# Two gate projections as seven half-size products each, with weight factors made in the first scan and the first gate as a pass of its own

## The chip, the core and the metric

The kernel runs on one core of a Trainium2 chip. The metric is the device time of one execution in microseconds (us). Engines are named as the profile does: PE is TensorE, PEld its weight loads, DVE is VectorE, ACT is ScalarE, POOL is GpSimd, SP the engine from whose queue all DMAs of this kernel are issued.

## What is computed

One layer of a mixer with two parallel recurrent branches over 16 meta tokens and 2048 tokens of width 1024, in float32. Cut to what matters here:

```python
h = concat([meta_tokens, x])                  # 2064 x 1024
xn = rmsnorm(h, norm_w)
proj = xn @ w_in                              # 1024 x 6152
a_q, a_k, a_v, a_beta, a_alpha, a_z, b_q, b_f, b_i, b_g, gate_a, gate_b = split(proj)
y_a = gated_delta_net(conv(a_q, a_k, a_v), a_beta, a_alpha) * silu(a_z)   # 4 heads of 128, chunked scan
y_b = hgrn2(b_q, b_f, b_i) * silu(b_g)                                    # 4 heads of 128, chunked scan
mixed = sigmoid(gate_a) * (y_a @ w_branch_a) + sigmoid(gate_b) * (y_b @ w_branch_b)
out = rmsnorm(h + mixed @ w_out, final_norm_w)[16:]
```

`gate_a` and `gate_b` are two projections of 1024 columns each from the same normalised tokens.

## The kernel before

Tokens are worked on in 17 chunks of 128; chunk 0 holds the meta tokens, the 16 others go in 8 pairs. Each float32 operand of a projection is kept as two float16 tiles, a high and a low part, and a product is three matmuls per block of 128 rows: high by high, high by low, low by high (`SPLITS`, L251). A projection of 512 columns for one chunk is then 8 x 3 = 24 matmuls into one PSUM bank (`tok_major`, L253).

The work runs in three stages.

- **First scan** (L708 to L749): normalise and transpose the tokens of a pair (`xprep`) and store them in device memory (`xs_d`, L712); run the second branch's recurrence (`levels`, `scan1`) with its four projections. In it the generator `bg` prepares the weights for the second scan, two steps per chunk (L744), placed behind marks of the scan's own instructions by `issue_after`.
- **Second scan** (L1056 to L1102): convolution and recurrence of the first branch, one `stage` and one `scan2` per chunk, both with raised priority (`AHEAD`).
- **Merges** (L1183): per chunk two branch products (`branch`, L797), the scaled sum, a split into float16 parts, transposes, the output product (L1172) and the last norm.

Weights are prepared by `prepare` (L221): load 2 MB, take a scale from the largest squares (`stats_steps`, L185), then in 8 steps (`split_steps`, L204) scale on VectorE, copy the high part on ScalarE (L216) and subtract it on VectorE or GpSimd (L217). They lie in a ring of six buffers, tag `w`, which also holds the two pair tiles of the second scan.

The gates are made in the third place, for every chunk by itself: `gate` (L353) takes two projections of 512 columns per gate, and ScalarE applies tanh as it takes the bank (L360). Their four weights are begun in the last pairs of the second scan (L1072, L1077, L1085). The gates of chunks 1 to 3 are made at the end of that scan (in pieces of 256 columns), and their first branch right after it (L1103); the merge loop makes the gates of a chunk three chunks ahead (L1186). The weights of the branches and of the output product are prepared around the end of the second scan (L1102, L1124 to L1127).

Instructions are written in program order with priorities. A scheduler orders each engine's queue by a simulated timeline; on the chip each queue then runs in that order, and an instruction that waits holds up those behind it. PSUM tags of the second and third stage: `d`, `e`, `s`, `o` with two banks each (`BANKS`, L32); gate products use `d`, branches `e`, transposes and output products `s`.

## Time and profile before

| | |
|---|---|
| runs | 1903.33, 1904.47 and 3626.0 us, median 1904.47 |
| profiled execution | 1903.0 us, span of its instructions 1901.2 us |
| TensorE busy | 1774.5 us, 93%, 17247 matmuls |
| VectorE busy | 1202.5 us, 63% |
| ScalarE busy | 881.9 us, 46% |
| GpSimd busy | 311.6 us, 16% |
| mean granted clock of TensorE | 0.973 |
| DMA | 105 MB, 55 GB/s in the mean |

The page gives the busy share of each engine and of 40 equal slices of the span (digits are tenths). Groups of instructions are named by line, engine, operation and tiles, with count, total and mean duration. The chain is followed back from the last instruction to what released each step. Windows give the busy time of each engine in a stretch, with the clock that TensorE was granted as a share of 2.4 GHz. TensorE's matmuls overlap, so the distance between starts says more of their cost than their duration.

### The profile page before, as it was taken

The page shows a single profiled execution, that of the slowest core. Times are in us where ns is not written, and L with a number is a line of the kernel's source. Part 1 is how long each engine was busy: PE and PEld are TensorE (multiplying, and loading weights), DVE is VectorE, ACT ScalarE, POOL GpSimd, SP SyncE. Part 2 cuts the span into 40 slices and gives each one's busy share as a digit, 9 for nine tenths or more (in the row PEclk, how much of TensorE's full clock was granted, in tenths as well). Part 3 has the DMA queues.
Part 4 walks back from the last instruction along what each step waited for, and adds up shares of the span by engine and source line. Part 5 has one row for each costly group of instructions (what it writes and reads, how often), then busy time and mean ns, then how long its engine had stood idle before and what let it go on. Part 6 is the DMA issues. An engine that isn't in the chain of part 4 may idle for free.

```text
span 1901.2 us, 43142 instructions
## 1 busy us (share of the span) xinstructions
PE 1774.5 (93%) x17247; PEld 1215.1 (64%) x17247; DVE 1202.5 (63%) x5070; ACT 881.9 (46%) x2208; POOL 311.6 (16%) x441
## 2 busy tenths in 40 slices
PE   4599999999986899999999998888999999999998
PEld 3476767777665788788888876764444444444444
DVE  7954765667579788988988989758222333242344
ACT  7654665566576445655556686753111111111111
POOL 3300111112115212212212145322000000000000
PEclk9699999999988899999999998999999999999999
DMA  9111111010300001000000132240111111211011
GB/s 334 41 50 41 57 52 52 13 46 35 118 30 12 29 24 35 24 29 30 13 29 11 56 115 93 76 153 25 67 56 34 61 50 39 72 45 34 33 51 45
DMA packets 38733, 105.05 MB, mean 55 GB/s; under 512 B 4156, under 2 KB 4340, under 8 KB 35460
## 3 DMA queue, kind: packets, MB, share of 16 engines
q1 hardware_dynamic: 38532, 102.29, 15.4%
q8 instruction: 135, 2.21, 0.5%
q14 instruction: 66, 0.54, 0.1%
HBM read 77.12 MB, written 25.17 MB: 54 GB/s over the span
## 4 chain that ended last, share of the span: by engine, by line
PE 70%; DVE 17%; ACT 7%; issue 3%; DMA 1%; POOL 1%; SPq 0%; ACTq 0%; POOLq 0%; DVEq 0%
PE pgate L259 16%; PE pc L267 10%; PE pout L1172 9%; PE pbr L806 7%; PE pq L267 5%; PE pzg L259 4%; PE pi L259 3%; PE pg L259 3%; DVE wsc L213 3%; DVE pair L318 2%; PE pkq L869 1%; PE pl L576 1%; DVE Y L901 1%; DVE R L899 1%; POOL yp L639 1%
## 5 line engine op out<-in xcount | busy, mean ns | idle before, releaser
L259 PEld LDWEIGHTS <-x 128*128 128x128 f16 x3192 | 311.4, 99 | 256.3 <-issue 8.4
L259 PE MATMUL pgate<-w_ga,x 128*128 128x512 f16 (+1 forms) x912 | 179.3, 352 | 6.6 <-POOL w_ga L217 2.8
L259 PE MATMUL pgate<-w_gb,x 128*128 128x512 f16 (+1 forms) x912 | 170.2, 345 | 0.0
L1172 PE MATMUL pout<-w_o,mt 128*128 128x512 f16 (+1 forms) x792 | 169.3, 373 | 0.2 <-ACT mt L1160 0.2
L318 DVE SCALAR_TENSOR_TENSOR pair<-raw,cw,pair 128x256 f32<-128x256 f32 (+1 forms) x297 | 140.5, 500 | 3.0 <-ACT pair L312 2.2
L806 PEld LDWEIGHTS <-y 128*128 128x128 f16 x768 | 75.5, 99 | 93.9 <-issue 8.3
L1172 PEld LDWEIGHTS <-mt 128*128 128x128 f16 x792 | 77.3, 98 | 88.6 <-DVE mt L1162 0.5
L1174 DVE SCALAR_TENSOR_TENSOR hres<-pout,mm,hres 128x512 f32<-128x512 f32 (+1 forms) x33 | 24.2, 734 | 165.3 <-PE pout L1172 165.3
L806 PE MATMUL pbr<-w_bra,y 128*128 128x512 f16 x384 | 89.7, 384 | 4.4 <-DVE mix L808 2.0
L259 PE MATMUL pi<-w_bi,x 128*128 128x512 f16 x408 | 92.5, 379 | 0.0
L267 PE MATMUL pq<-x,w_bq 128*128 128x256 f16 x768 | 89.2, 276 | 0.0
L267 PEld LDWEIGHTS <-w_aq 128*128 128x128 f16 x864 | 77.0, 100 | 16.8 <-POOL w_aq L217 4.5
L259 PE MATMUL pg<-w_bg,x 128*128 128x512 f16 x384 | 87.7, 379 | 0.0
L806 PE MATMUL pbr<-w_brb,y 128*128 128x512 f16 x384 | 87.4, 382 | 0.0
L267 PEld LDWEIGHTS <-w_ak 128*128 128x128 f16 x864 | 76.6, 98 | 13.7 <-issue 2.8
L553 DVE TENSOR_TENSOR QK<-QK,Tb 128x1024 f32<-128x1024 f32 x48 | 61.0, 1270 | 36.9 <-PE pl L581 36.9
L267 PEld LDWEIGHTS <-w_av 128*128 128x128 f16 x864 | 76.6, 99 | 12.0 <-issue 1.7
L901 DVE TENSOR_TENSOR Y<-Y,R 128x2 f32<-128x2 f32 (+14 forms) x510 | 83.9, 197 | 0.0
L267 PEld LDWEIGHTS <-w_bq 128*128 128x128 f16 x768 | 76.1, 99 | 9.4
L899 DVE TENSOR_TENSOR R<-R,U 128x2 f32<-128x2 f32 (+14 forms) x510 | 81.5, 193 | 0.3
L267 PE MATMUL pq<-x,w_bf 128*128 128x256 f16 x672 | 79.9, 273 | 0.0
L1175 ACT ACTIVATE mix<-hres 128x512 f32<-128x512 f32 x22 | 13.8, 629 | 129.2 <-DVE hres L1174 82.3
(470 smaller groups left out, 3672.7 us busy)
## 6 DMA issues: line engine op xcount, KB each, us to landing
x<-xs_d SPq DMA_DIRECT2D x14, 1024.0 KB, 4.7
hx<-in_x_dram SPq DMA_DIRECT2D x16, 512.0 KB, 3.4
xs_d<-x SPq DMA_DIRECT2D x8, 1024.0 KB, 3.9
hres<-in_x_dram SPq DMA_DIRECT2D x16, 512.0 KB, 3.5
out_dram<-hres SPq DMA_DIRECT2D x16, 512.0 KB, 2.6
yb_d<-yt SPq DMA_DIRECT2D x16, 256.0 KB, 2.0
ya_d<-yt SPq DMA_DIRECT2D x16, 256.0 KB, 2.0
y<-ya_d SPq DMA_DIRECT2D x16, 256.0 KB, 2.6
```

The lines of the kernel that those rows point to most:

```text
L213: E.tensor_scalar(t, raw[:, k, :], rows[:, k:k + 1], sc[:, 0:1], ALU.mult, ALU.mult)
L259: T.matmul(po[:, j:j + cols], xt[:, k, xa, c0:c0 + P], wt[:, k, wa, j:j + cols], start=(n == 0), stop=(n == 23))
L267: T.matmul(po, wt[:, k, wa, h * P:(h + 1) * P], xt[:, k, xa, c0:c0 + ncol], start=(n == 0), stop=(n == 23))
L318: V.scalar_tensor_tensor(av, rows(h, j), wv(j), av, ALU.mult, ALU.add)
L553: V.tensor_tensor(qk, qk, dv, ALU.mult)
L576: T.matmul(pd[a:a + 32, 2 * h + i], K[:, a:a + 32], Q[:, a:a + 32].rearrange("p (m z t) -> p m z t", z=2, t=s)[:, :, 1], start=True, stop= ...
L639: G.tensor_tensor(yp[:, 1], y, yp[:, 0], ALU.subtract)
L806: T.matmul(pb, y[:, h, xa, :], w[0][:, 4 * i + h, wa, :], start=(n == 0), stop=(n == 11))
L899: V.tensor_tensor(R[:, e, c:], R[:, e, c:], U[:, e, c:c + 1].broadcast_to([P, n // 2, 16 - c]), ALU.mult)
L901: V.tensor_tensor(Y[:, e, c:], Y[:, e, c:], R[:, e, c:], ALU.add)
L1172: T.matmul(po, mt[:, xa, k, :], wo[i][0][:, k, wa, js], start=(n == 0), stop=(n == 23))
L1174: V.scalar_tensor_tensor(h[:, i, js], po, mm[:, 2 + i:3 + i], h[:, i, js], ALU.mult, ALU.add)
```

## The change

Each gate of a pair of chunks (256 tokens by 1024 by 1024) is cut in two along all three sizes, and the four blocks of the result are put together from seven products of 128 tokens by 512 by 512 (Strassen's scheme in Winograd's form) instead of eight. Each product is 4 x 3 = 12 matmuls into one bank.

- `gate_steps` makes seven weight factors per gate from the four blocks of its weight and stores them in device memory (`wg_d`). Its steps run in the first scan, three per chunk from the second pair on, beside the two of `bg`. The raw weight is loaded twice (once for the scale), into one buffer of 1 MB.
- `left` makes the four sums of the token blocks for a pair, stores them (`ss_d`) in the first gate's pass and loads them in the second gate's.
- `gate_pair` runs seven products; ScalarE takes the first bank, VectorE adds the others into four float32 blocks, and ScalarE applies tanh in place.
- `first_gate` runs for the first gate: pairs 0 and 1 in the last two chunks of the second scan, pairs 2 to 7 after it, with nine steps of the four last weights behind each. The results go to device memory (`ga_d`). The merges load them again.
- `second_gate` runs in the merge loop, one pair ahead. The early gates and the early branches of chunks 1 to 3 fall away.

```diff
-    def gate(c, xt, which, t, parts=(0, 1)):
-        c0 = ((c - 1) % 2) * P
-        for i in parts:
...
-            tok_major(pg, xt, c0, wsl[n][0], 256 if c < 4 else 512)
-            A.activation(t[:, i, :], pg, AF.Tanh, scale=hu[:, j:j + 1])
+    def gate_steps(i, off, pool):
+        src = w_in[0][:, off:off + D].rearrange("(a k p) (b n) -> p k a b n", a=2, p=P, b=2)
...
+        def load(k):
+            t = gx.tile([P, 2, 2, 512], F32, tag="t8", name="graw")
+            for a in range(2):
+                SY.dma_start(t[:, a], src[:, k, a])
+            return t
+        for k in range(4):
+            t = load(k)
...
+            if k % 2:
+                V.tensor_reduce(st, t.rearrange("p a b n -> p (a b) n"), AX.X, ALU.max, apply_absolute_value=True)
...
+            else:
+                for j in range(4):
...
+                    A.activation(junk, t[:, j // 2, j % 2], AF.Square, scale=rows[:, j // 2, k:k + 1],
+                                 accum_out=st[:, j:j + 1])
+            yield
...
+        for k in range(4):
+            t = load(k)
+            for a in range(2):
+                A.activation(t[:, a], t[:, a], AF.Copy, scale=fac[:, a, k:k + 1])
+            def put(n, b, f):
+                o = pool.tile([P, 2, 512], F16, tag="go", name="go", bufs=3)
+                A.activation(o[:, 0], b, AF.Copy, scale=f)
+                if f == 1.0:
+                    V.tensor_tensor(o[:, 1], b, o[:, 0], ALU.subtract)
+                else:
+                    V.scalar_tensor_tensor(o[:, 1], b, f, o[:, 0], ALU.mult, ALU.subtract)
+                SY.dma_start(wg_d[i][:, ORDER.index(n), k], o)
...
+            put("P1", b11, 1.0)
+            put("P2", b21, 1.0)
+            put("P3", b22, 2.0)
+            yield
+            V.tensor_tensor(b11, b12, b11, ALU.subtract)
+            put("P5", b11, 2.0)
+            V.tensor_tensor(b12, b22, b12, ALU.subtract)
+            put("P7", b12, 2.0)
+            yield
+            V.tensor_tensor(b22, b22, b11, ALU.subtract)
+            put("P6", b22, 2.0)
+            V.tensor_tensor(b21, b21, b22, ALU.subtract)
+            put("P4", b21, 1.0)
+            yield
+    def left(q, first):
+        x = xpair(q)
+        S = mp.tile([P, 4, 4, 2, P], F16, tag="xm", name="xs", bufs=2)
+        if not first:
+            SY.dma_start(S, ss_d[q])
+            return x, S
...
+        def put(n, s):
+            A.activation(S[:, n, :, 0], s, AF.Copy, scale=0.5)
+            V.scalar_tensor_tensor(S[:, n, :, 1], s, 0.5, S[:, n, :, 0], ALU.mult, ALU.subtract)
...
+        V.tensor_tensor(s, a(1, 0, 0), a(1, 1, 0), ALU.add)
+        V.tensor_tensor(t, a(1, 0, 1), a(1, 1, 1), ALU.add)
+        V.tensor_tensor(s, s, t, ALU.add)
+        put(0, s)
+        for h in range(2):
+            V.tensor_tensor(s, s, a(0, 0, h), ALU.subtract)
+        put(1, s)
+        for h in range(2):
+            V.tensor_tensor(s, a(0, 1, h), s, ALU.subtract) if h == 0 else V.tensor_tensor(s, s, a(0, 1, h), ALU.add)
+        put(3, s)
+        u, t = tmp("s3"), tmp("s3l")
+        G.tensor_tensor(u, a(0, 0, 0), a(1, 0, 0), ALU.subtract)
+        G.tensor_tensor(t, a(0, 0, 1), a(1, 0, 1), ALU.subtract)
+        G.tensor_tensor(u, u, t, ALU.add)
+        put(2, u)
+        SY.dma_start(ss_d[q], S)
+        return x, S
+    def gate_pair(i, xS, w, t):
...
+        def prod(n):
+            po = psd("pgate")
+            m = 0
+            for k in range(4):
+                for (xa, wa) in SPLITS:
+                    T.matmul(po, L[n](k, xa), w[ORDER.index(n)][:, k, wa], start=m == 0, stop=m == 11)
+                    m += 1
+            return po
+        def add(po, *ds):
+            with tc.high_priority(offset=OFS):
+                for d, s in ds:
+                    V.tensor_tensor(d, s, po, ALU.add)
+        def end(d):
+            A.activation(d, d, AF.Tanh, scale=hu[:, i:i + 1])
+        po = prod("P1")
+        with tc.high_priority(offset=OFS):
+            A.activation(c21, po, AF.Copy)
+        add(prod("P2"), (c11, c21))
+        end(c11)
+        add(prod("P6"), (c12, c21))
+        add(prod("P7"), (c21, c12))
+        add(prod("P5"), (c12, c12), (c22, c21))
+        end(c22)
+        add(prod("P3"), (c12, c12))
+        end(c12)
+        add(prod("P4"), (c21, c21))
+        end(c21)
+    def first_gate(q):
...
+        gate_pair(0, left(q, True), wga, t)
+        for j in range(2):
+            SY.dma_start(ga_d[2 * q + 1 + j], t[j])
...
                         run_steps(bg, LAST[i] if last else 2)
+                        if not last:
+                            run_steps(gsteps, 3)
             if p == 0:
+                gsteps = chain(gate_steps(0, OFF_GA, p1), gate_steps(1, OFF_GB, p1))
...
                         if p == NP_ - 2:
-                            run_steps(bg, 13)
-                            bg2 = gate_begin("gb0")
+                            wga = [f for j in range(4) for f in gate_part(0, j, wp if j < 3 else gx)]
                 else:
-                    bg3 = gate_begin("gb1")
-                    run_steps(bg2)
...
+                    first_gate(i)
...
+        wgb = gate_part(1, 0, wp)
+        bg = chain(prepare(beg["bra"], "bra", ((), EVEN)), prepare(beg["brb"], "brb", ((), EVEN)),
+                   prepare(beg["o0"], "o0", (HALF, EVEN)), prepare(beg["o1"], "o1", (HALF, EVEN)))
+        for q in range(2, NP_):
+            first_gate(q)
+            run_steps(bg, 9)
+        run_steps(bg)
+        wgb += [f for j in (1, 2, 3) for f in gate_part(1, j, wp if j < 3 else gx)]
...
+        def second_gate(q):
+            gate_pair(1, left(q, False), wgb, [tbs[:, (2 * q + j) % 4] for j in range(2)])
+        def merge(c, tb):
+            mix = raw_t("mix").rearrange("p h i -> p (h i)")[:, :D].rearrange("p (a n) -> p a n", a=2)
+            SY.dma_start(mix, ga_d[c])
+            branch(c, ya_d, wba, mix)
...
-        for c in range(1, NCH):
-            merge(*ready.pop(0))
-            if c + 3 < NCH:
-                ready.append(gates(c + 3))
+        second_gate(0)
+        for q in range(NP_):
+            if q + 1 < NP_:
+                second_gate(q + 1)
+            for j in range(2):
+                merge(2 * q + 1 + j, tbs[:, (2 * q + j) % 4])
```

`gate_part(i, j, pool)` loads two of the stored factors (one for the last j) into a buffer of the ring `w`, or into the buffer of `gate_steps` for the last. The factors lie in the order P1, P2, P6, P7, P5, P3, P4. The branch inputs `y` have two buffers instead of three.

## Rows read from the trace of the kernel before

**Rows 1.** The page's part 1, TensorE; part 2, TensorE in 40 slices.
```profile
PE 1774.5 (93%) x17247; PEld 1215.1 (64%) x17247; DVE 1202.5 (63%) x5070; ACT 881.9 (46%) x2208; POOL 311.6 (16%) x441
...
PE   4599999999986899999999998888999999999998
```
**Rows 2.** The page's part 4, the chain that ended last, by line.
```profile
PE pgate L259 16%; PE pc L267 10%; PE pout L1172 9%; PE pbr L806 7%; PE pq L267 5%; PE pzg L259 4%; PE pi L259 3%; PE pg L259 3%; DVE wsc L213 3%; DVE pair L318 2%; PE pkq L869 1%; PE pl L576 1%; DVE Y L901 1%; DVE R L899 1%; POOL yp L639 1%
```
**Rows 3.** Pieces of that chain, 1440 to 1485 us: start, us, what.
```profile
1445.91 10.36 PE pgate L259 x48
1456.27 0.89 PE mT L1158 x16
```
**Rows 4.** Windows: stretch, length, busy us (count) of the engines, clock, DMA.
```profile
1120.00:1320.00 200.00, 174.59 (x1490) 127.73 (x1489) 162.67 (x681) 120.90 (x310) 77.43 (x87) 0.93 0.26 92
...
1335.00:1850.00 515.00, 515.00 (x2530) 239.37 (x2529) 152.78 (x320) 75.83 (x122) 0.00 (x0) 1.00 0.15 50
1850.00:1901.20 51.20, 42.31 (x242) 22.03 (x239) 25.81 (x64) 8.45 (x16) 0.00 (x0) 0.97 0.11 42
```
**Rows 5.** Windows of 60 us in the first scan, one pair each.
```profile
130.00:190.00 60.00, 60.00 (x871) 43.60 (x870) 29.03 (x78) 30.79 (x59) 4.30 (x3) 1.00 0.12 42
...
370.00:430.00 60.00, 59.25 (x849) 43.59 (x842) 38.21 (x116) 37.45 (x77) 8.91 (x7) 1.00 0.10 37
430.00:490.00 60.00, 56.80 (x842) 41.78 (x840) 40.34 (x112) 35.69 (x71) 13.26 (x9) 1.00 0.17 63
```
**Rows 6.** Groups by line with shapes apart, ScalarE; then line 200's instructions.
```profile
L406 ACT ACTIVATE x<-hx,rx 128x1024 f16<-128x1024 f32 x17 | 19.6, 1164 | 5.1 <-DVE rx L403 5.1
...
L200 ACT ACTIVATE junk<-w_gb,nw 128x512 f16<-128x512 f32 x16 | 11.6, 722 | 1.4 <-DMA w_gb<-in_w_in_dram 1.4
...
L216 ACT ACTIVATE w_gb<-wsc 128x512 f16<-128x512 f32 x16 | 9.8, 624 | 3.9 <-DVE wsc L213 3.8
...
L200 ACT ACTIVATION_READ_ACCUMULATOR junk<-w_ga,nw x16: 185/188/213, 1084.3 to 1106.6; 128x1 f32 x16
```
**Rows 7.** Timeline of VectorE at 1273 us: start, us, instruction.
```profile
1273.25 0.68 DVE L217 TENSOR_TENSOR w_bra<-wsc,w_bra 128x512 f16<-128x512 f32 x1
1273.85 0.15 DVE L195 TENSOR_TENSOR stats<-stats 128x2 f32<-128x2 f32 x1
```
**Rows 8.** Waits of TensorE, 190 to 490 us: total, times, longest.
```profile
PE yT L643 <- ACT yp L638: 3.3, 2, 1.7
PE pl L581 <- DVE QK L553: 3.2, 4, 1.0
```
**Rows 9.** DMA issues: size and median us to landing.
```profile
w_ga<-in_w_in_dram SPq DMA_DIRECT2D x4, 1024.0 KB, 7.3
```
**Rows 10.** Windows of w_ga's, then w_gb's instructions: PE, DVE, ACT, POOL.
```profile
1085.00:1260.00 175.00, 40.52 (x288) 6.48 (x8) 22.19 (x46) 22.79 (x24) 0.94 0.25 90
...
1085.00:1260.00 175.00, 31.69 (x274) 9.62 (x16) 22.33 (x48) 18.65 (x16) 0.94 0.25 90
```
**Rows 11.** Windows of pgate's (PE, ACT), then pbr's (PE, DVE) instructions.
```profile
1120.00:1320.00 200.00, 84.31 (x624) 8.19 (x12) 0.93 0.26 92
...
1120.00:1320.00 200.00, 35.50 (x144) 7.61 (x12) 0.93 0.26 92
```
**Rows 12.** Line 217, two of its groups: ns min/median/max, first to last start.
```profile
L217 POOL TENSOR_TENSOR w_o<-wsc,w_o x8: 1155/1246/1467, 1289.0 to 1310.0; 128x512 f16<-128x512 f32 x8
L217 DVE TENSOR_TENSOR w_o<-wsc,w_o x8: 671/681/1653, 1289.2 to 1309.3; 128x512 f16<-128x512 f32 x8
```
**Rows 13.** Timeline of VectorE in one merge.
```profile
1414.69 1.29 DVE L1143 SCALAR_TENSOR_TENSOR mix<-tb,us,mix 128x1024 f32<-128x1024 f32 x1
...
1424.36 0.69 DVE L1162 COPY mt<-mT 128x1024 f16<-128x1024 f16 x1 [4.06 <-PE mT L1158]
```
**Rows 14.** Windows of 50 and of 10 us, for the clock.
```profile
450.00:500.00 50.00, 47.21 (x733) 32.38 (x732) 29.64 (x56) 23.16 (x50) 11.31 (x7) 1.00 0.26 97
...
1130.00:1140.00 10.00, 6.36 (x25) 5.04 (x24) 9.61 (x53) 6.36 (x19) 6.17 (x7) 0.66 0.00 0
```

More of the change, by code (lines that the diff above doesn't have):

```diff
@@ L30 @@
 AHEAD = 1500
-EARLY = 3
 BANKS = (dict(d=3, e=2, s=2, o=1), dict(d=2, e=2, s=2, o=2))
@@ L160, in load_small, with scale_of @@
         return cw, gna, gnb, hb
-    def scale_of(stats, nt, tag):
+    def scale_of(stats, nt, tag, exp=WS_EXP):
         sc = cp.tile([P, 2], F32, name=f"sc_{tag}")
@@ L247, in hybrid_kernel @@
     yb_d = [dp.tile([P, H, 2, P], F16, name=f"yb_d{c}") for c in range(NCH)]
+    wg_d = [dp.tile([P, 7, 4, 2, 512], F16, name=f"wg_d{i}") for i in range(2)]
+    ss_d = [dp.tile([P, 4, 4, 2, P], F16, name=f"ss_d{q}") for q in range(NP_)]
+    ga_d = [dp.tile([P, 2, 512], F32, name=f"ga_d{c}") for c in range(NCH)]
     uy = cp.tile([P, 2], F32, name="uy")
@@ L278, in hybrid_kernel @@
     G.memset(hist, 0.0)
-    hu = cp.tile([P, 4], F32, name="hu")
+    hu = cp.tile([P, 2], F32, name="hu")
     def conv(n, xt, pidx, dst, later=False, tag=None):
@@ new lines, in gate_part, with a, tmp @@
+    def gate_part(i, j, pool):
+        n = 2 if j < 3 else 1
+        t = pool.tile([P, 2 * 4, 2, 512] if n == 2 else [P, 4, 2, 512], F16, tag="w" if n == 2 else "t8", name=f"wg{i}{j}")
+        SY.dma_start(t.rearrange("p (f k) a n -> p f k a n", k=4), wg_d[i][:, 2 * j:2 * j + n])
+        return [t[:, 4 * f:4 * f + 4] for f in range(n)]
+    def left(q, first):
[4 more added lines that the diff above has]
+            return x, S
+        def a(i, j, h):
+            return x[:, 4 * j:4 * j + 4, h, P * i:P * i + P]
+        def put(n, s):
+            A.activation(S[:, n, :, 0], s, AF.Copy, scale=0.5)
+            V.scalar_tensor_tensor(S[:, n, :, 1], s, 0.5, S[:, n, :, 0], ALU.mult, ALU.subtract)
+        def tmp(n):
+            return sp.tile([P, 512], F32, tag="st", name=n).rearrange("p (k i) -> p k i", k=4)
+        s, t = tmp("s1"), tmp("s1l")
+        V.tensor_tensor(s, a(1, 0, 0), a(1, 1, 0), ALU.add)
[15 more added lines that the diff above has]
+        return x, S
@@ L364, in hybrid_kernel @@
+    def first_gate(q):
+        t = [raw_t("gt0").rearrange("p h i -> p (h i)")[:, :D], acc_t("gt1")]
+        t = [x.rearrange("p (a n) -> p a n", a=2) for x in t]
+        gate_pair(0, left(q, True), wga, t)
+        for j in range(2):
+            SY.dma_start(ga_d[2 * q + 1 + j], t[j])
     bw = gp.tile([P, KT, 2, 2 * H], F16, name="bw")
@@ L1051, in xpair_mid @@
                 return xpair(p)
-            t = mp.tile([P, KT, 2, 2 * P], F16, tag="xm", name="xm")
+            t = mp.tile([P, KT, 2, 2 * P], F16, tag="xm", name="xm", bufs=2)
             SY.dma_start(t, xs_d[p])
@@ L1070, in hybrid_kernel @@
                         conv("q", xn, p + 2, pn["q"])
-                        if p == NP_ - 2:
-                            bg = chain(gate_begin("ga0"), gate_begin("ga1"))
                     else:
@@ L1112, in hybrid_kernel @@
         SY.dma_start(fnw, final_norm_w.rearrange("(o d) -> o d", o=1).broadcast_to([P, D]))
-        def gates(c):
-            if c % 2 == 1:
-                xg[c] = xg[c + 1] = xpair((c - 1) // 2)
-            t = gate_tiles(c)
-            for w in range(2):
-                gate(c, xg[c], "ab"[w], t[w])
-            return c, *t
-        beg["o0"], beg["o1"] = out_begin(0, wx), out_begin(1, wx)
-        run_steps(prepare(beg["brb"], "brb", ((), EVEN)))
-        wba, wbb = wsl["bra"], wsl["brb"]
-        run_steps(prepare(beg["o0"], "o0", (HALF, EVEN)))
-        run_steps(prepare(beg["o1"], "o1", (HALF, EVEN)))
-        wo = [wsl["o0"], wsl["o1"]]
+        beg["bra"] = br_begin(w_branch_a, gna, "bra")
+        beg["brb"] = br_begin(w_branch_b, gnb, "brb")
+        beg["o0"], beg["o1"] = out_begin(0, wx), out_begin(1, wx)
+        wgb = gate_part(1, 0, wp)
[6 more added lines that the diff above has]
+        wgb += [f for j in (1, 2, 3) for f in gate_part(1, j, wp if j < 3 else gx)]
+        tbs = wp.tile([P, KT, 2, 512], F16, tag="w", name="tbs")
+        tbs = tbs.rearrange("p k a n -> p (k a n)").bitcast(F32).rearrange("p (c a n) -> p c a n", c=4, a=2)
+        wba, wbb, wo = wsl["bra"], wsl["brb"], [wsl["o0"], wsl["o1"]]
         us = p1.tile([P, 4], F32, name="us")
@@ L1134, in hybrid_kernel @@
             V.tensor_scalar(uo[:, i:i + 1], wo[i][1], XS / MS, None, ALU.mult)
-        def merge(c, mix, tb):
-            if c > EARLY:
-                branch(c, ya_d, wba, mix)
+        def second_gate(q):
[4 more added lines that the diff above has]
+            branch(c, ya_d, wba, mix)
             h = acc_t("hres").rearrange("p (a n) -> p a n", a=2)
```

69 lines of the change are left out of this document (25 added, 44 removed).

## The prediction

> **What bounds the kernel now.** I read the page's engine shares first: TensorE is busy 93% of the span, VectorE 63%, and the slices show TensorE at 9 nearly everywhere except at the start, around 600 us and around 1150 to 1320 us [rows 1]. In the chain that ended last the lines with the largest shares are all TensorE's, the gate product (L259) first [rows 2]. Busy TensorE is not TensorE at its peak, so next come the pieces of that chain in the last third: 48 matmuls of 512 columns take 10.36 us, 215.8 ns each, and they follow one another without a gap [rows 3]. From 1335 to 1850 us TensorE is busy 515.00 of 515 us at clock 1.00 [rows 4]: here each matmul left out is worth its 215.8 ns.
>
> Between 1120 and 1320 us it is otherwise: TensorE is idle for 25.4 us of 200 and granted 0.93 of its clock, which costs some 14 us more, while VectorE works 162.7 us of it [rows 4]. I call these 39 us the lost time of the seam between second scan and merges. In the first scan a pair of chunks takes 60 us; the pair without weight preparation beside it leaves TensorE no idle time, the five after it 1.9 us each on average (0.75 in the best of the five, 3.2 in the last), with VectorE busy near 39 us and ScalarE near 36 [rows 5].
>
> **The change part by part.** *Matmuls removed.* Each gate of a pair of chunks was 2 chunks x 2 halves x 24 = 96 matmuls of 512 columns; seven half-size products of 12 make 84. Over 8 pairs and 2 gates that is 1536 against 1344, and 192 x 0.2158 = 41.4 us go. (The first three chunks ran as 256 columns, twice as many; I count them as the same columns.) The gates take 331.5 us of TensorE now and 290.1 after, 18.13 us per gate and pair.
>
> *Weight factors in the first scan.* Per gate: 8 loads of 1 MB (each part twice, as two DMAs), then per part 2 scalings of 1024 elements on ScalarE, 7 copies there, and 11 VectorE operations of 512 (4 differences, 7 second halves). ScalarE: 8 squares of 0.72 + 0.19, 4 x (2 x 1.16 + 7 x 0.63) [rows 6], together 34 us. VectorE: 44 x 0.60 (start to start in a run without gaps [rows 7]; an operation alone is shown at 0.68; no sum of two f16 tiles into f32 is in the trace, I take the f32 ones') + 2 reductions of 2048 elements at 4 x 0.60 each + small ones, some 33 us. Both gates: ScalarE +68, VectorE +66. The 32 steps are issued three per chunk from the second pair on, so spread over 5.5 pairs: per 60 us VectorE goes from 39 to 51, ScalarE from 36 to 48. Neither is full, so no throughput is lost; what remains is an in-order queue standing on one of the new operations while TensorE needs the next. The trace shows this kind: TensorE waited for the ScalarE copy before the transposes (3.3 us) and for the level products' decay on VectorE (3.2 us) in these pairs [rows 8]. Bounds: nothing, and the present idle time scaled by ScalarE's background work (4.1 us a pair now, from 16 squares and 16 copies over six pairs, 12.4 more: 1.9 x 3.0 = 5.7 a pair, 34 us in all). I take another 1.9 a pair on six pairs, 12 us, since VectorE and ScalarE keep 9 and 12 us of slack per pair and the new work waits for no GpSimd operation, as the present does. The DMAs (32 loads of 512 KB, 56 stores of 256 KB) add 30 MB to 330 us; 1 MB of these weights lands in 7.3 us in the median [rows 9] and the queue is far from full, so I give them nothing.
>
> *The seam.* Out of it go the gates' preparation (VectorE 6.5 + 9.6 us [rows 10] and some 5 us of small operations), the early branches and the first merge's vector work (some 15 us): 162.7 - 36 = 127 us of VectorE stay, of which some 42 are the four last weights. In come eight first-gate passes. One has 11 VectorE operations in `left` (7 sums, 4 second halves) and 7 additions from PSUM, 18 x 0.60 = 10.8 us, eight passes 86. So VectorE has 213 us to do. TensorE's own work there: 200 - 39 = 161 us at full clock, less the gates of chunks 1 to 3 and half of chunk 4 (576 of 256 columns and 48 of 512: 72.6) and 144 branch matmuls (31) [rows 11], leaves 57, and 8 x 18.13 = 145 come in: 202 us. VectorE is the bound by a little; with 4% of waits I let the stretch last 222 us, to 1342. The lost time there becomes 20 instead of 39, a gain of 19. Bounds: 202 (TensorE loses nothing) to 241 (it loses 39 us as before); with every VectorE operation at 0.68 it would be 225. The first two passes can't run through early: the part with P5 and P3 goes to a buffer that a pair tile holds, as w_gb's did; that is why I give nothing for a better fill of the second scan's end.
>
> The Trainium skill has a rule that speaks against this part (SBUF — State Buffer, "SBUF: two separate sides"): a VectorE operation with two SBUF inputs and a GpSimd operation share a port pair as a lock, and the later one stands still. The trace bears it out: w_o's subtraction took 0.68 us in the median but up to 1.65 beside GpSimd's of 1.25 [rows 12]. By the rule the 24 GpSimd sums of `left` (1.16 to 1.25 each) could cost VectorE up to 29 us; but 41.4 us of GpSimd work on the gate weights leave the same stretch [rows 10], so by it the sum would come out up to 12 us lower, not higher.
>
> *The merges.* After the seam TensorE has 8 second gates (145.0) and 16 merges, each two branches and the output product at 96 x 0.2158 and 0.89 of transposes, 21.61, 345.8 together [rows 3]: 490.8 us. VectorE: 152.8 us in 515 now [rows 4], some 26 us per pair, plus 4.8 for additions, in a period that shrinks from 84.7 us (2 x (192 x 0.2158 + 0.89)) to 61.3: half busy. New waits: the additions wait for a product, on VectorE, and TensorE for the bank two products later. Behind a waiting addition stand the merge's chain (L1143, L1145, L1153, 1.2 to 1.3 us each, some 9.7 us until the transposes' copies [rows 13]), which was covered by a gate's 10.36 us and now is by the other chunk's branches or the gate. A bank must be free 2.59 us after its product; the addition takes 0.68 after at most one operation of 1.3. I give 0.5 us a pair, 4 us; bounds none and 87 (last rival). The loads of factors, sums and stored first gates (some 20 MB more over these 490 us) run ahead of their use by a pair. The end keeps its 8.9 us of idle [rows 4].
>
> **Sum.** 1120 + 222 + 491 + 4 + 9 = 1846, and 12 of the first scan: 1858 us of span; the same by differences, 1901.2 - 41.4 - 19 + 4 + 12 = 1857. The profiled execution took 1903.0 us with a span of 1901.2, so 1860; the median of the runs, 1904.47, lies 1.5 above it: 1861 us, 2.3% less.
>
> **Rivals.** *The fill closes the seam:* VectorE is faster than counted, the first scan hides all. Then TensorE alone counts: 1120 + 202 + 491 + 9 = 1822, and 1825 with the 1.8 and 1.5 us of the sum. For it: the first scan's slack, GpSimd's relief; against: 213 against 202 us of counted work.
>
> *The first scan pays:* its queues stall in proportion, 34 us instead of 12, and the seam costs its upper bound, 19 more: 1861 + 22 + 19 = 1902, no change. For it: 1.9 us of idle time came with the present, smaller background work. Against: the longest of those waits was 1.7 us [rows 8].
>
> *The drains set the pace* (slower): in the 16 passes each product's drain lies bare, because VectorE comes to the addition later than 2.59 us after the product's end, when its other bank is also full. Place: psum tag d, two banks; price per pass: six single drains and one double, 8 x 0.68 = 5.4 us, 87 in all: 1861 - 4 + 87 = 1944, 2.1% above. For it: the stretch of first gates has VectorE nearly full. Against: in the merges VectorE is half idle and the additions go ahead of other work. The Trainium skill would make it dearer (TensorE: Matmul & The Clock Gate, "A second HAM failure mode: psum-queue depth-cycling"): small idle moments between groups that cycle through PSUM banks made the clock swing between its levels. The trace doesn't bear that out so far: with 2.8 us of small idle moments in 50, at 450 to 500 us, the granted clock stayed 1.00 (2.4 GHz), and it showed 0.66 where TensorE had stood idle 3.64 us of 10 [rows 14]; at 1.2 GHz the passes would take another 290 us if it stayed down.
>
> **Chances.** Forecast 0.50 (1842 to 1882 for it alone), closed seam 0.17, first scan pays 0.21, drains 0.12. About 2%, 38 us, is what a measurement of this kernel tells from no change; the bound lies at 1866, inside the forecast's own range, which I split 0.34 to 0.16. Faster by over 2%: 0.34 + 0.17 = 0.51; slower by over 2%: 0.09 of the last case (its dearer part); within 2%: the rest, 0.40. The range goes from the closed seam's 1825 to the first scan's 1902.
>
> **What would show it.** Right: 1344 gate matmuls; a stretch of 12 of them at 2.59 us; merges with a period near 61 us and no idle TensorE; the seam's end near 1342 plus what the first scan added; pairs of the first scan at 62 us. Wrong: TensorE waiting for VectorE's additions more than 0.5 us a pair (then the drains rule), pairs of the first scan above 66 us with ScalarE or VectorE named as releaser, or DMA named before a factor product.

## The result, and the profile after

The changed kernel takes 1930.0 us in the median (1924.0 to 1931.8), the kernel before 1903.9: a ratio of 1.0138, 95% interval 1.0114 to 1.0162. That is slower by 1.4%, where I forecast 2.3% faster, and above the range I gave. The profiled execution took 1930.5 us with a span of 1928.7, 27.5 longer than before. Three executions in a slower state of the chip (3626.0 us of the kernel before, 2624.8 and 1943.5 in two experiments) enter no ratio here.

The page of the kernel after, its parts 1, 2 (40 slices) and 5 (groups); the first answers to [rows 1]:

```profile
PE 1747.4 (91%) x16763; PEld 1178.6 (61%) x16763; DVE 1360.7 (71%) x5340; ACT 932.3 (48%) x2264; POOL 305.2 (16%) x425
...
PE   4599898969999689999999999987789999999997
...
PEclk9699899979998889999999999988889999999999
...
L459 PE MATMUL pgate<-wg,xs 128*128 128x512 f16 x768 | 186.3, 397 | 32.5 <-ACT xs L422 29.7
...
L459 PE MATMUL pgate<-wg,x 128*128 128x512 f16 x576 | 132.5, 382 | 4.4 <-ACT gt L472 2.9
```

The matmuls went as counted: 768 + 576 = 1344 gate products instead of 1536 of the same width. The slices show where the time went all the same: the digits of TensorE fall to 7 and 8 in slices 27 to 29 (1250 to 1400 us), with the clock at 8, and three of the slices between 190 and 434 us fall to 8, 8 and 6 where all were 9. The group of the products with sums (`xs`) names a wait of 29.7 us that the kernel before did not have.

Windows of the kernel after (columns as in [rows 4]): two pairs of the first scan, the seam, the merges.

```profile
190.00:250.00 60.00, 47.31 (x741) 37.65 (x738) 44.25 (x129) 41.52 (x79) 5.59 (x4) 0.89 0.33 115
370.00:430.00 60.00, 42.50 (x605) 31.69 (x593) 34.32 (x111) 37.87 (x85) 4.42 (x3) 0.83 0.36 120
1250.00:1300.00 50.00, 44.94 (x343) 25.98 (x343) 42.91 (x200) 24.72 (x58) 16.29 (x15) 0.90 0.36 134
1300.00:1350.00 50.00, 38.88 (x181) 18.16 (x179) 38.42 (x71) 20.85 (x45) 15.60 (x11) 0.86 0.48 177
1350.00:1400.00 50.00, 37.16 (x161) 16.26 (x160) 30.20 (x48) 19.21 (x39) 9.44 (x7) 0.86 0.38 139
1400.00:1450.00 50.00, 40.67 (x177) 17.90 (x176) 28.46 (x44) 12.72 (x20) 9.52 (x7) 0.90 0.80 300
1450.00:1850.00 400.00, 400.00 (x2004) 187.42 (x2002) 193.58 (x389) 70.09 (x112) 0.00 (x0) 1.00 0.29 97
```

The merges are as forecast: TensorE busy 400 of 400 us at clock 1.00, no drain bare. The pairs of the first scan, which lost 1.9 us each [rows 5], now leave TensorE idle 12.7 and 17.5 us in the two worst stretches, though VectorE and ScalarE are *less* busy there than I had allowed (44 and 34 us, 42 and 38, against 51 and 48). In the seam VectorE, which I had called the bound, works 28 to 38 us of 50 from 1300 to 1450 us while TensorE is idle for 9 to 13 of them (from 1250 to 1300 us it works 42.9, with TensorE idle for 5.1). Neither loss looks like one of throughput.

One mark cuts the 27.5 us in two: the start of the second scan's first key-query product (`pkq`), at 636.4 us before and 693.3 after. The first scan is 56.9 us longer (forecast 12); all behind it is 29.4 shorter (forecast 41.4 + 19 - 4 = 56.4). So 45 us of the miss lie in the first scan and 27 behind it. Up to the mark TensorE runs the same 7674 matmuls, first before, then after:

```profile
0.00:636.40 636.40, 552.17 (x7674) 411.98 (x7674) 429.75 (x1182) 384.58 (x815) 131.29 (x118) 0.95 0.19 68
0.00:693.30 693.30, 571.51 (x7674) 427.42 (x7674) 497.60 (x1300) 444.06 (x919) 128.45 (x118) 0.90 0.32 111
```

Of the 56.9 us, 37.6 are idle time of TensorE (121.8 against 84.2) and 19.3 are its matmuls running longer, with the granted clock at 0.90 of 2.4 GHz instead of 0.95 in the mean.

**The seam, read.** Timeline of TensorE in the kernel after, then of VectorE over the same time (start, us, instruction, and in brackets the idle time before it and its releaser):

```profile
1367.34 5.34 PE L459 MATMUL pgate<-wg,x 128*128 128x512 f16 x24 [0.66 <-DVE gt L466]
1384.87 13.31 PE L459 MATMUL pgate<-wg,xs 128*128 128x512 f16 x48 [12.19 <-ACT xs L422]
```

```profile
1366.60 0.69 DVE L466 TENSOR_TENSOR gt<-gt,pgate 128x512 f32<-128x512 f32 x1 [1.90 <-PE pgate L459]
...
1367.85 1.27 DVE L214 TENSOR_SCALAR wsc<-w_o,sc_o 128x512 f32<-128x512 f32 x3
...
1375.58 0.68 DVE L428 TENSOR_TENSOR s<-x 128x512 f32<-128x512 f16 x1
...
1376.90 1.52 DVE L429 TENSOR_TENSOR s1l<-x 128x512 f32<-128x512 f16 x1
1378.45 1.52 DVE L430 TENSOR_TENSOR s<-s,s1l 128x512 f32<-128x512 f32 x1
```

TensorE has run P1 and P2, which need only tokens, and stands 12.19 us idle until the first sum is there. VectorE had been waiting for TensorE just before (1.90 us idle at 1366.60); then it scales a weight for 8 us, and only after that begins the sums of the pair that TensorE is on. In program order `left(q+1)` stands behind the nine weight steps of pass q.

**The first scan, read.** Four queues of the kernel after at 237 to 249 us: SP, ScalarE, VectorE, TensorE.

```profile
237.81 1.31 SPq L354 DMA_DIRECT2D graw<-in_w_in_dram  x2
```

```profile
242.64 1.15 ACT L377 ACTIVATE graw<-graw,gfac 128x1024 f32<-128x1024 f32 x1 [3.48 <-DMA graw<-in_w_in_dram]
```

```profile
244.86 1.41 DVE L383 TENSOR_TENSOR go<-graw,go 128x512 f16<-128x512 f32 x1 [4.97 <-ACT go L381]
...
247.11 1.22 DVE L682 TENSOR_TENSOR QK<-QK,Tb 128x1024 f32<-128x1024 f32 x1
```

```profile
248.38 0.74 PE L705 MATMUL pl<-QK 128*32 128x16 f32 x64 [2.50 <-DVE QK L682]
```

From the page, the issues of this load (last number: us from issue to landing, median); then, over the whole run, how long ScalarE and VectorE stood on it (us, times):

```profile
graw<-in_w_in_dram SPq DMA_DIRECT2D x32, 512.0 KB, 5.0
  DMA graw<-in_w_in_dram: 26.2, 11
```

A part of the gate weight is asked for in the middle of a chunk's steps, when its one buffer comes free; ScalarE's scaling of it waits 3.48 us; VectorE stands 4.97 us on the half that needs ScalarE's; and behind that stands the next level's product of the recurrence, for which TensorE waits. The scheduler had put gate operations between the levels.

### The profile page after: what moved, and what is told of

Its sections match the earlier page's. It is cut to its first block, busy times and chain, and to the rows that moved or that the text cites. A ratio compares the mean times of both kernels' runs of the same rounds, so it can differ in the third digit from the quotient of the medians.

```text
span 1928.7 us, 42889 instructions
## 1 busy us (share of the span) xinstructions
PE 1747.4 (91%) x16763; PEld 1178.6 (61%) x16763; DVE 1360.7 (71%) x5340; ACT 932.3 (48%) x2264; POOL 305.2 (16%) x425
## 5 line engine op out<-in xcount | busy, mean ns | idle before, releaser
L459 PE MATMUL pgate<-wg,xs 128*128 128x512 f16 x768 | 186.3, 397 | 32.5 <-ACT xs L422 29.7
L259 PEld LDWEIGHTS <-x 128*128 128x128 f16 x1368 | 131.7, 99 | 94.9 <-issue 3.3
L459 PEld LDWEIGHTS <-xs 128*128 128x128 f16 x768 | 77.0, 102 | 127.5 <-ACT xs L422 31.7
L459 PE MATMUL pgate<-wg,x 128*128 128x512 f16 x576 | 132.5, 382 | 4.4 <-ACT gt L472 2.9
L459 PEld LDWEIGHTS <-x 128*128 128x128 f16 x576 | 56.6, 99 | 71.4 <-issue 6.7
L682 DVE TENSOR_TENSOR QK<-QK,Tb 128x1024 f32<-128x1024 f32 x48 | 61.4, 1279 | 23.4 <-PE pl L710 23.4
```

The lines of the kernel that those rows point to most:

```text
L259: T.matmul(po[:, j:j + cols], xt[:, k, xa, c0:c0 + P], wt[:, k, wa, j:j + cols], start=(n == 0), stop=(n == 23))
L459: T.matmul(po, L[n](k, xa), w[ORDER.index(n)][:, k, wa], start=m == 0, stop=m == 11)
L682: V.tensor_tensor(qk, qk, dv, ALU.mult)
```

## The experiments

Theories on record: for the first scan, in-order queues standing on the new operations (arithmetic), against the transfers; for the seam, VectorE's order against its throughput. All runs are compared with the kernel before on the same chip (medians 1902.4 to 1904.2). The runs were on five chips, so a difference between two of them can be off by a microsecond or two.

**Parts of the first scan alone**, on the kernel before. The first run adds `gate_steps` and its calls as in the change; the factors are used by nobody.

> The kernel before with the 32 gate steps added to its first scan and nothing else of the change (the factors are stored and not used). If the first scan is what costs the kernel after some 50 us: 1904 + 50, 1940 to 1965 us, the start of the second scan some 50 us later than before. If my 12 us were right and the loss sits elsewhere: 1910 to 1922 us.

1952.3 us, ratio 1.0250 (1.0224 to 1.0276): the first scan alone costs 48.

```diff
-                SY.dma_start(t[:, a], src[:, k, a])
+            return stats16[0]
...
-                SY.dma_start(wg_d[i][:, ORDER.index(n), k], o)
```

> As the kernel with the gate steps alone, but without their DMAs: the steps work on one zeroed tile that stays, and nothing is loaded or stored. Theory (the in-order queues of VectorE and ScalarE stand on the new arithmetic, in program order, while TensorE needs the next operation behind it): most of the 50 us stays, 1935 us or more. Rival (the queues stand on the DMAs: the single load buffer, the three output buffers, SP's stores ahead of the token loads): 1920 us or less.

(Both cut from the edit; `stats16[0]` is here a tile set to zero once.) 1936.2 us (1.0150 to 1.0184): the arithmetic alone costs 32.

The other half keeps the two kinds of `dma_start` and drops everything between them.

> The other half: the 32 loads and 56 stores of the gate steps in their places, without the arithmetic (the stores take one zeroed tile). Theory (arithmetic): 1904 to 1910 us. Rival that the DMAs by themselves take something from the first scan (queue of SP, ports): 1915 us or more.

1909.8 us (1.0014 to 1.0039): the transfers alone cost 5.6, with nobody waiting for their data. Beside the arithmetic they cost 16. Two last runs split these: without the loads (the first minus line above), and without the stores (the second).

> The kernel with the gate steps alone (1952.3), without the 32 loads (the steps work on one zeroed tile that stays); the 56 stores and all arithmetic remain, three steps per chunk. With arithmetic alone it was 1936.2, with all 1952.3. If the loads into the one buffer are what the transfers add: 1934 to 1940 us. If the stores (three output buffers, SP's queue) are: 1947 us or more.

1923.9 us (1.0090 to 1.0124), faster than either band.

> The same kernel with its 32 loads and without its 56 stores, so that the factors are made and not kept. If the stores are what the transfers add: 1934 to 1940 us. If the loads are: 1947 us or more.

1949.0 us (1.0224 to 1.0255). Taken out of the whole, the loads are worth 28 of the 48 us and the stores 3; with the stores gone already, the loads are worth 13 (1949.0 against 1936.2). The waits of TensorE on the levels' products, 190 to 690 us, first with all, then without loads, then without stores (total, times, longest):

```profile
PE pl L640 <- DVE QK L617: 13.7, 4, 7.4
PE pl L645 <- DVE QK L617: 12.5, 7, 4.2
```

```profile
PE pl L642 <- DVE QK L619: 4.8, 5, 2.1
PE pl L647 <- DVE QK L619: 3.7, 4, 1.4
```

```profile
PE pl L639 <- DVE QK L616: 10.7, 4, 6.6
...
PE pl L644 <- DVE QK L616: 8.0, 6, 1.8
```

26.2 us become 8.5 without the loads and 18.7 without the stores; with the arithmetic alone they are 6.1, so most of its 32 us are not this chain, and I did not read where they lie. One thing does not add up: with the stores gone as well as the loads (1936.2) it was 12 us slower than with the stores kept (1923.9). Each edit makes the scheduler order the queues anew; a dozen microseconds in these runs can come from that order, and I read no smaller difference as a mechanism.

**The seam.** The sums one pair ahead:

```diff
+        xS = left(2, True)
         for q in range(2, NP_):
-            first_gate(q)
+            nxt = left(q + 1, True) if q + 1 < NP_ else None
+            first_gate(q, xS)
             run_steps(bg, 9)
+            xS = nxt
```

> The kernel after with the sums of a pair's token blocks written one pair ahead, in front of the gate products and of the nine steps of weight preparation of the pass before. Theory (VectorE's order: the sums stand behind the weight steps and TensorE waits for them): the waits of the products for the sums, 29.7 us at the seam, go for the most part, 1900 to 1910 us. Rival (VectorE's throughput, GpSimd beside it or the token loads bound the seam): 1922 us or more.

1913.6 us (1.0031 to 1.0064), 16.5 less than the kernel after: above the theory's band, well below the rival's. Its waits of TensorE, 1150 to 1450 us:

```profile
PE np L166 <- ACT junk L199: 12.5, 1, 12.5
PE pgate L459 <- DVE gt L466: 10.3, 12, 3.1
```

The 29.7 us for `xs` are gone, and a new wait of 12.5 stands there: the small matmul that sums a weight's statistics.

> The kernel with the sums a pair ahead, and with 8 instead of 9 steps of weight preparation behind each pass, so that the output weights' steps begin only behind the fourth pass. In the run with the sums ahead TensorE stood 12.5 us on one small matmul for a weight's scale, whose squares waited for w_o's load. If that wait is what was left of the seam: 10 to 12 us less than 1913.6, 1902 to 1904 us. If something else takes its place (the chain of sums, additions): no less than 1911 us.

1918.2 us (1.0066 to 1.0096): a miss. Fewer steps per pass did not move the wait, which grew to 13.6. Its TensorE, ScalarE and SP queues show why:

```profile
1376.26 0.59 PE L166 MATMUL np<-stats,k 128*128 128x8 f32 x2 [13.55 <-ACT junk L199]
1376.71 8.19 PE L459 MATMUL pgate<-wg,x 128*128 128x512 f16 x24
```

```profile
1370.51 0.63 ACT L199 ACTIVATE junk<-w_o 128x512 f16<-128x512 f32 x1 [6.74 <-DMA w_o<-in_w_out_dram]
```

```profile
1362.07 4.94 SPq L181 DMA_DIRECT2D w_o<-in_w_out_dram  x4
```

The output weight is loaded at 1362.07, when the second scan has left its memory. The scheduler placed its statistics and their matmul as if the load took less, ahead of products that ran without a wait as soon as it was done (1376.71). So the place has to be given by hand:

```diff
-            run_steps(bg, 8)
+            if q < 5:
+                run_steps(bg, 8)
-        run_steps(bg)
+        with tc.issue_after(mark["gT"].ins), tc.issue_after(mark["gV"].ins), tc.issue_after(mark["gA"].ins):
+            run_steps(bg)
```

(the marks are the last matmul, addition and tanh of the last pass)

> The kernel with 8 steps, and the two output weights' preparation queued behind the last first-gate pass on TensorE, VectorE and ScalarE. In the run with 8 steps TensorE still stood 13.6 us on the scale's small matmul, since w_o can only be loaded once the second scan has left its buffers. If nothing takes the place of that wait: 10 to 13 us less than 1918.2, 1905 to 1908 us. Rival (the wait moves into the first merge, whose output product now comes before its weight is ready): 1914 us or more.

1908.6 us (1.0019 to 1.0042), 9.6 less, just short of the 10 to 13 I expected. TensorE still waits 5.9 us there. Last, on the best first scan (below, 1874.8 us), `second_gate(0)` is written ahead of these steps:

> The kernel with both gates' statistics in the first pair (1874.8), with the first pass of the second gate written in front of the output weights' preparation, so that their scale's small matmul, for which TensorE still stood 5.9 us after the last first-gate pass, stands behind 18 us of products. If that wait goes: 4 to 6 us less, 1869 to 1871 us. If the first output product then waits for its weight: no gain.

1859.8 us, ratio 0.9777 (0.9753 to 0.9801): the best version, 2.2% faster than the kernel before and 15 less than its base, more than the 5.9 us of the wait. Between the two profiled executions it is 13.6, and 5.6 of these lie before the second scan, where nothing was edited. Its seam (stretch and columns as above) and its largest wait of TensorE from 1130 to 1430 us:

```profile
1300.00:1350.00 50.00, 46.03 (x218) 21.63 (x217) 40.08 (x70) 20.62 (x38) 15.25 (x11) 0.97 0.61 225
1350.00:1400.00 50.00, 48.90 (x241) 22.65 (x240) 23.83 (x38) 16.12 (x34) 0.00 (x0) 1.00 0.83 328
```

```profile
PE pgate L460 <- DVE gt L467: 9.2, 9, 2.9
```

**The place of the steps in the first scan**, on the kernels with the seam mended. Queueing the steps behind the last level of their pair:

```diff
+                if p > 0 and not last:
+                    with tc.issue_after(mark["EA"].ins), tc.issue_after(mark["EV"].ins):
+                        run_steps(gsteps, 3 if i == 0 else 3)
```

(in place of the call behind `bg`'s steps; the marks are ScalarE's last copy and VectorE's last product of the levels)

> The same kernel (sums ahead, 8 steps) with the gate steps of the first scan queued behind the last level of their pair on VectorE and ScalarE, so that few of them stand between two levels' operations. Nothing is left out. Theory (the order: operations of the steps stand in the chain of levels and make it longer than TensorE's other work covers): the 32 us that the arithmetic costs fall to 10 or less, so 20 us or more below the run with 8 steps. Rival (throughput of VectorE and ScalarE, 12 us a pair wherever they stand): within 6 us of it.

1959.9 us (1.0283 to 1.0317), 42 *more*. My first theory, that moving them from among the levels would take the cost away, fell here; whether a place among the levels costs something by itself, the run does not say. ScalarE's timeline in this run:

```profile
227.65 1.15 ACT L377 ACTIVATE graw<-graw,gfac 128x1024 f32<-128x1024 f32 x1 [5.59 <-DMA graw<-in_w_in_dram]
230.55 1.15 ACT L377 ACTIVATE graw<-graw,gfac 128x1024 f32<-128x1024 f32 x1 [1.75 <-DMA graw<-in_w_in_dram]
...
233.17 0.67 ACT L588 ACTIVATE qx<-pq,sc_bq 128x512 f32<-128x512 f32 x1
```

ScalarE stands 5.59 and 1.75 us on the load with the copy of the next projection (`qx`) behind it: the steps stand in front of other work now, and the loads are as bare as before (ScalarE's scalings wait 19.2 us for them in this run, 12.6 in the kernel after).

> As the kernel with the steps behind the levels, and the 56 stores of the factors issued from ScalarE's queue instead of SP's, so that SP's later loads no longer stand behind stores that wait for VectorE. If SP's order is the 6 to 16 us that the DMAs cost (alone and beside the arithmetic): 5 us or more faster than the run before. If the wait for an output buffer or the load's own time is it: no gain, or some us slower because ScalarE now waits for VectorE's half of each factor.

`SY.dma_start(wg_d...)` became `A.dma_start(...)`: 1968.4 us (1.0316 to 1.0362), 8.6 more than its base. This gives the theory of SP's order no support; it does not rule it out, since ScalarE's queue now waits for VectorE's half of each factor, but without any stores (above) only 3 us were gained.

> The kernel with the output weights late, whose first scan leaves out the statistics of the gate weights: 16 of the 32 loads, 16 squares, four reductions; the scale comes from a constant. Theory now: three statistics steps in a row expose three loads, each into the one buffer of 1 MB, and ScalarE and VectorE stand on them with TensorE's copies behind (the two worst minutes of the run with the steps behind the levels, 190 to 250 and 370 to 430 us, are those two stretches). Then 20 us or more less than the kernel with the output weights late. Rival (the differences and halves in the chain of levels are the cost): less than 10 us less.

1870.2 us (0.9812 to 0.9841), 38 less than its base. Its first scan is only 10 us longer than that of the kernel before, with the seven factors of both gates made in it. The window of one of its pairs:

```profile
190.00:250.00 60.00, 58.26 (x832) 42.71 (x830) 50.20 (x138) 46.98 (x90) 9.92 (x6) 1.00 0.42 147
```

VectorE at 50 and ScalarE at 47 of 60 us, as forecast (51 and 48), and TensorE keeps 58 of 60; over five such windows, 190 to 490 us, it keeps 56.8 of 60. Throughput is out as a rival. The statistics were four steps in front of each gate's parts. Does their work cost 38 us, do their loads, or their place?

> The kernel with the output weights late (1908.6), its statistics steps working on a resident constant in the same places and sizes, so that their 16 loads are left out (the scale then comes from the constant). Theory (ScalarE and VectorE stand on the statistics' loads): most of the 38 us of the run without statistics comes back, 1870 to 1882 us. Rival (the arithmetic of the statistics, its 2.3 us reductions and the scale's matmul in the queues): 1895 us or more.

1902.9 us (0.9988 to 1.0010): 6 less. The theory fell: without the 16 loads of the statistics most of the 38 us stay, and 6 is no more than I grant to a new order. What also stays is the grouping. With three steps per chunk and four steps ahead, each chunk runs the last step of one part and the first two of the next, whose load is asked for in mid-chunk.

```diff
+SLOTS = (4, 3, 3, 3, 3, 4, 3, 3, 3, 3, 0, 0)
-                            run_steps(gsteps, 3)
+                            run_steps(gsteps, SLOTS[2 * p - 2 + i])
```

> The kernel with the output weights late (1908.6) with one edit: each gate's four statistics steps run in one chunk, so that every later chunk's three steps are one whole part, its load first; begin, order, arithmetic and loads stay. Before, chunks 2 to 5 of each gate ran the last step of one part and the first two of the next, whose load waits for the one buffer in the middle of the chunk's steps. If that load in the middle is the cost (pairs of 73 to 77 us where the run without statistics has 61 to 67): 1876 to 1886 us. Rival (the statistics steps cost by their own work and waits): 1898 us or more.

1887.2 us (0.9891 to 0.9944), 21 less, all statistics and loads kept. It lies just above the band I gave the theory and well under the rival's. How long the two engines stood on the load and VectorE on ScalarE's half (us, times), first in the base, then here:

```profile
  DMA graw<-in_w_in_dram: 24.3, 10
  DVE go L383: 22.1, 8
```

```profile
  DMA graw<-in_w_in_dram: 20.2, 10
  DVE go L384: 12.6, 6
```

So the grouping is worth 21 us, but the loads themselves are waited for nearly as long as before. What shrank is the wait behind them: VectorE's for ScalarE's half by 9.5 us, and TensorE's for the levels' products (190 to 690 us) from 24.7 to 18.9. That the load in mid-chunk is the cause fits this; it is argued, not shown. The edit also ends the steps a chunk earlier, but the gain lies in pairs 2 to 4 (below).

Four other places, by a table of steps per chunk (per pair: 1 1 3 3 2 3 3, and the same behind the levels; 2 3 3 2 3 3 0; and 4 3 3 3 3 with both gates' statistics first). In all four the gate steps are also written ahead of `bg`'s in their chunk, and the last gives two small tiles a second buffer:

> The kernel with the output weights late, with all its statistics, but one statistics step per chunk instead of three (two for the second gate), beginning a pair earlier; three part steps per chunk as before. Theory (exposed loads of the statistics): 10 us or more less than the kernel with the output weights late. Rival (the part steps cost): within 5 us of it.

1900.4 us (0.9976 to 0.9995), 8 less than its base: between the theory's 10 and the rival's 5.

> As the kernel with one statistics step per chunk, and the steps queued behind the last level of their pair, as in the run that came out at 1959.9. If that run's loss was its statistics in bursts alone, and the order in the chain of levels matters too: faster than the run with one per chunk. If standing behind the levels is itself worse (ScalarE's and VectorE's copies for the next projections stand behind the steps): slower than it by 10 us or more.

1907.0 us (1.0012 to 1.0031), 6.6 more than the run before: in neither band.

> The kernel with one statistics step per chunk, begun in the first pair with two per chunk and otherwise three steps per chunk, so that all steps end a pair earlier (before the last pair but one). In the run with one per chunk (1900.4) the first four pairs lost little and the last two 12 and more us. If late part steps beside the second scan's first work are what was left: 1880 to 1890 us. Rival (statistics cost wherever they stand): 1898 us or more.

1882.0 us (0.9878 to 0.9910), as expected.

> The statistics of both gates in the first pair, four steps per chunk, where no weight preparation runs and ScalarE and VectorE are busy 31 and 30 us of 60; then the part steps exactly where the run without statistics has them. If the free engines of that pair take the waits on the loads: within 12 us of 1870. If ScalarE or VectorE standing on a load costs TensorE's time there as well: 8 loads of some 5 us each, 1890 us or more.

1874.8 us (0.9842 to 0.9873), as expected, and 34 less than with the output weights late, all work kept. The pairs themselves, by the starts of one instruction of VectorE that comes once a pair (`QK<-qx,ff`) in the timelines; us from one to the next for pairs 2 to 6, their sum, and the start of the second scan (the execution without loads that is shown took 1931.5 us, 7.6 above that run's median):

| kernel | pairs 2 to 6 | sum | second scan |
|---|---|---|---|
| before | 62.9 60.2 60.8 62.2 56.6 | 302.7 | 636.4 |
| after | 76.4 73.4 77.1 69.3 62.1 | 358.3 | 693.3 |
| arithmetic alone | 72.7 66.0 64.8 72.2 57.3 | 333.0 | 665.1 |
| without loads | 72.9 66.6 63.2 65.1 59.0 | 326.8 | 660.9 |
| without statistics | 61.3 66.6 66.0 59.8 57.5 | 311.2 | 646.8 |
| aligned | 66.6 64.5 69.2 67.6 64.3 | 332.2 | 668.5 |
| statistics first | 68.0 69.2 67.3 64.6 56.7 | 325.8 | 665.5 |

With whole parts in every chunk a pair costs 57 to 69 us; in the kernel after, pairs 2 to 4 cost 73 to 77. TensorE over pairs 2 to 5 (windows, columns as above), first in the kernel before, then before and after the alignment:

```profile
217.40:463.50 246.10, 239.20 (x3485) 175.48 (x3484) 155.73 (x450) 148.03 (x302) 41.93 (x29) 1.00 0.10 38
```

```profile
217.50:514.50 297.00, 262.59 (x3562) 189.30 (x3554) 215.03 (x555) 196.01 (x379) 41.76 (x31) 0.93 0.33 114
```

```profile
219.10:487.10 268.00, 246.18 (x3477) 181.66 (x3476) 208.88 (x545) 194.64 (x381) 38.21 (x28) 0.96 0.37 126
```

Of the 51 us that these pairs are longer without the alignment, 27.5 are idle time of TensorE (34.4 against 6.9); the alignment gives back 12.6 of them. The other 23.4 us are not all clock, though its mean is 0.93 here: the marks are VectorE's, and between them TensorE runs 77 matmuls more. The whole first scan, with equal matmuls, tells what the clock cost: in the kernel after 19.3 us beside 37.6 of idle time, about half a microsecond for each one of waiting.

Three things stay open. Pair 2 takes 73 us without any load too (the rows "arithmetic alone" and "without loads"), so something besides the load costs there: the grouping, or the work itself. And the one-per-chunk table, aligned as well, gains little (1900.4): its parts run up to a pair later, nearer to the second scan's first work, and the table that ends a pair earlier is 18 faster; which work they meet there I did not separate. And a second load buffer, which might take the wait itself away, was not tried: that the single buffer sets the loads' price is argued from the waits, not shown.

## Why the prediction was wrong, step by step

- *"192 x 0.2158 = 41.4 us go"*: right, 1344 products, and merges with TensorE busy 400 of 400 us.
- *"The DMAs ... the queue is far from full, so I give them nothing"*: this step failed. I priced the loads by bandwidth, and put the time until they land at nothing. One buffer of 1 MB is asked for when its last reader is done; each half lands 5.0 us after its issue in the median, and two in-order engines stood on it for 26.2 us. Without loads 28 of the 48 us were gone, or 13 where the stores were gone already. The transfers alone, with nobody waiting, cost 5.6.
- *"Neither is full, so no throughput is lost; what remains is an in-order queue standing on one of the new operations ... I take another 1.9 a pair on six pairs, 12 us"*: the mechanism was named rightly and the first half shown (50 and 47 us of 60, TensorE at 58); the size was not. With its loads the first scan is the larger part of the miss, 45 of 72 us: it grew by 56.9 us (55.6 of them in five pairs) instead of 12, beyond my upper bound of 34 as well. I priced a wait by its idle time alone: TensorE's idle time grew by 37.6, and the lower clock took 19.3 more. The arithmetic without loads, which is nearest to what I priced, costs 20 to 32 by the runs, not 12. The reason I gave for the low value, that the new work waits for no GpSimd operation, overlooked that it waits for a DMA. Without statistics the whole came to 10 us, near the 12; with half of the loads and part of the arithmetic left out there, that does not confirm it.
- *"VectorE is the bound by a little; with 4% of waits I let the stretch last 222 us"*: failed. The stretch (from 1120 + 56.9 to the last first-gate addition, at 1437) lasted some 261 us, beyond my bound of 241, with 201 us of VectorE's work in it where I had counted 213. The work was counted about rightly; the wait was not. The sums stood behind weight steps, in an order that the diff shows (`left` inside `first_gate`, `run_steps(bg, 9)` behind it): I summed the engine's work and never asked in what order TensorE would need it. From the second scan's start to the end I forecast 56.4 us less than the 1264.8 of before, 1208; after has 1235, the version with the statistics first and the output weights late 1210.5 (its profile, 1876.0 - 665.5), the best one 1202.5 (1862.4 - 659.9). The gain was there; the order kept it.
- *"I give 0.5 us a pair"* for bare drains, and the rival with the drains: the seam's waits for additions are 4.2 us in all, the merges have none, as I gave. Where the sums came in time, the seam's grew to 11.6 us (output weights late) and 9.2 (the best version), over the 4 I gave and far under the rival's 87, so the rival is out. The granted clock stayed at 1.00 over the 400 us of merges. The case of the Trainium skill (TensorE: Matmul & The Clock Gate, "A second HAM failure mode: psum-queue depth-cycling") arises with small idle moments between the groups; TensorE had none there, so the trace neither bears it out nor speaks against it.
- The rule on the port pair (the Trainium skill: SBUF — State Buffer, "SBUF: two separate sides"): the trace agrees again, the sum at 1378.45 (L430) took 1.52 us while a GpSimd operation of 1.48 us ran from 1377.95, where the eight sums of this line take 0.69 in the median. It sets little here, since VectorE was not the bound.
- Of the rivals "the first scan pays" came nearest, at 1902; both of its halves were larger (57 us against 34, and 27 against 19).

## What to carry to other kernels

Work put into another stage's idle engines costs what stands *behind* it in their queues when it waits, not its busy time. So count, for each moved step, what it waits for and what stands behind it in its queue: here the same steps, grouped so that each load opens a chunk instead of falling into its middle, were 21 us faster, and with the statistics moved to a pair with free engines 34. Price a wait with the clock that it costs as well. In a stage that one engine bounds by a little, write down the order in which the bounding engine needs its operands before adding up anybody's work; and a small operation whose data come late (a scale's matmul) belongs, by hand if need be, behind products that are ready.

## What the runs showed that I had not expected

- Moving the same steps from between the levels to behind them made the kernel 42 us slower (1918.2 to 1959.9).
- The transfers alone cost 5.6 us and the arithmetic alone 32, but the arithmetic with the stores alone 20 and with the loads alone 45: the parts of one background job do not add.
- A first scan in which TensorE's idle time grew by 37.6 us ran its same matmuls at a mean granted clock of 0.90 instead of 0.95, and they took 19.3 us longer for it; a stretch with 17.5 us idle of 60 showed 0.83.
- A load's wait does not show at the load: it appeared as TensorE's wait on VectorE (`pl` for `QK`), two engines further on.
